# Layer A's group map multiplied into the u columns of the input projection on the chip, instead of a group product in every chunk

## Chip, cores and metric

The kernel runs on one core of one Trainium2 chip. The metric is the device time of one execution in microseconds, given as the median of several runs; a profiled execution, taken by the hardware profiler, has its own time.

## What is computed

A two-layer encoder trunk over 2048 tokens of width 1024. Layer 0 is the one that the change touches:

```python
def pool_mixer(h, w_in, w_group, scale, w_out):
    u, z = jnp.split(h @ w_in, 2, axis=-1)
    u = u.reshape(B, S, N_POOL_GROUPS, POOL_GROUP_DIM)      # 4 groups of 256
    cs = jnp.cumsum(u, axis=1)
    for g, w in enumerate((2, 4, 8, 16)):                   # trailing mean over w tokens
        means.append((cs[:, :, g] - cs shifted by w) / min(position, w))
    pooled = stack(means) - u
    mixed = einsum('bsgc,gcd->bsgd', pooled, w_group).reshape(B, S, 1024) * scale
    return (mixed * silu(z)) @ w_out
```

Here `h` is the RMS-normed input. The pooling works along the tokens and the group map along the channels of one group, so the two can change places: mapping u first and pooling afterwards gives the same values but for rounding. The layer's output is added to the stream, then a gated embedding `(p @ ple_w) * sigmoid(x @ ple_gate_w)` is added. A key/value projection follows, and layer 1 is a stick-breaking attention over 16 heads with its own projections.

## The kernel before, in words

All products run as three float32r matmuls (high x high, low x high, high x low): every operand is split into a rounded high part and a low remainder, a `pair` of two 128x512 tiles. Activations lie with channels on the partitions and 512 tokens along the free axis. `split` (L168) makes a pair: ACT copies the high part, another engine subtracts.

The first half of the program works on four chunks of 512 tokens, one after the other. A chunk is a list of 22 steps: for the groups 3, 2, 1, 0 a u step (`run_u`) and a z step (`run_z`), four steps of the output projection (`run_o`), four of the gated embedding (`run_g`), and six for q, k and v (`run_kvq`). One step's product of 1024 input channels is 8 x 2 x 3 = 48 matmuls of 128x512 on TensorE (`product`, L119). The weights of step i + 1 are requested before step i runs (L533), into a ring of 12 weight pairs (`wpair`, 512 KB each) that raw tiles (`wraw`, 3 of 256 KB) feed. `load_w` (L85) splits weights on ACT and DVE (L107, L108, with the norm's gain multiplied in) or ACT and POOL or DVE (L101, L103). The pairs of the layer's input projection are written to DRAM in the first chunk (L112, tensor `wi`), and later chunks load these pairs (L96).

A u step scales the product by the token's norm (`ub`, L230), forms the trailing sums in 1 to 4 shifted additions (`us`, L236, on DVE or POOL), takes mean minus itself (`po`, L240) and splits it into the pair `pp` (L247). The group product `run_m` (L268) multiplies `pp` by the group map, 2 x 2 x 3 = 12 matmuls of 128x512; it runs one u step later (for group 0 after the last z step). Its result is scaled, multiplied by SiLU(z) (`mf`, L275) and split into the pair `mp`, the operand of the output projection. `run_o` takes the `mp` pairs in the order 6, 7, 4, 5, 2, 3, 0, 1.

Beside the steps, the loads of the next chunk's input (`load_x`, `prep`) and the splitting of weights that the second half needs (`keep`, tiles `kraw` and `kpair`) are put in between. A scheduler orders the instructions of each engine within these dependences; an engine then runs its own list in order. SP issues most DMAs, also in order. The second half is the attention with layer 1's projections, from about 1415 us on.

## Time and profile before

| | us |
|---|---|
| median of 3 runs | 2865.52 |
| lowest, highest | 2864.01, 2867.44 |
| profiled execution | 2867.54 |
| its span, first to last instruction | 2865.7 |

The profile's page gives busy time by engine: PE is TensorE's matmuls, PEld its weight loads, DVE VectorE, ACT ScalarE, POOL GpSimd, SP the engine that issues DMAs. Further views used here: groups of instructions by line and shape (`line engine op out<-in shapes xcount | busy us, mean ns of one | idle time of the engine before them and what ended it`); windows (`from:to length, busy time and count by engine, clock, DMA share, GB/s`); waits (`engine line waited for: us in all, times, longest`); the timeline (`start us, duration us, engine, line, op, tiles, count`, in brackets the idle time before and what ended it). L353 is the line of the q, k, v products, L202 that of the input transposes, L598 and L599 are products of the attention, L623 its transposes.

### The profile page before, as it was taken

Reading aid. Unit: us, or ns where it says so; the run is one execution under the profiler, and the core shown is the slowest. Engines: PE = TensorE matmul, PEld = TensorE weight load, DVE = VectorE, ACT = ScalarE, POOL = GpSimd, SP = SyncE. Lnnn points to the kernel's source line nnn. Section 1 sums busy time; section 2 is a strip of 40 time slices with the busy share of each in tenths; the row PEclk is TensorE's granted clock in tenths of the full one; section 3 lists DMA queues with packets and bytes.
Section 4 is the critical chain, followed back from the end, with each engine's and each line's share of the span. In section 5 each row is a group of like instructions: output and inputs, shape, how many; then the busy total and the mean of one; then the engine's idle time right before and its main releaser. Section 6 shows DMA issues by size and latency. Waiting matters only on the chain. (4 is left out here: it accounts for less than half of the span.)

```text
span 2865.7 us, 40527 instructions
## 1 busy us (share of the span) xinstructions
PE 2763.3 (96%) x13667; PEld 2273.2 (79%) x13667; DVE 1893.8 (66%) x2581; ACT 1405.6 (49%) x2765; POOL 956.2 (33%) x965
## 2 busy tenths in 40 slices
PE   8899999999999999999899999999999999999999
PEld 6688788888888888888777888787877778878877
DVE  5645535455355543555299989999999988886642
ACT  4444523355234542345255555656566655554431
POOL 3464347542474425743212121221111122213220
PEclk9999999999999999999999999999999999999999
DMA  7756696467955678446657565555555556667765
GB/s 265 257 162 216 220 305 208 143 205 250 306 160 169 223 243 287 136 153 207 212 188 229 163 216 170 159 164 177 165 161 161 163 176 193 186 188 243 251 207 158
DMA packets 335139, 576.43 MB, mean 201 GB/s; under 512 B 32782, under 2 KB 161838, under 8 KB 334932
## 3 DMA queue, kind: packets, MB, share of 16 engines
q1 hardware_dynamic: 327944, 564.34, 61.2%
q10 hardware_dynamic: 6988, 9.50, 1.1%
q8 instruction: 108, 1.77, 0.3%
q14 instruction: 99, 0.81, 0.1%
HBM read 433.16 MB, written 132.19 MB: 197 GB/s over the span
## 5 line engine op out<-in xcount | busy, mean ns | idle before, releaser
L353 PE MATMUL psd<-wpair,x 128*128 128x512 f32 x2304 | 544.8, 393 | 0.0
L602 ACT ACTIVATE kap<-psl 128x512 f32<-128x512 f32 (+3 forms) x640 | 340.3, 533 | 407.6 <-PE psl L599 398.3
L609 DVE TENSOR_TENSOR_SCAN pp<-kap,pp,zeros 128x512 f32<-128x512 f32 x384 | 512.2, 1338 | 23.3 <-ACT kap L602 21.2
L353 PEld LDWEIGHTS psd<-wpair,x 128*128 128x128 f32 x2304 | 428.8, 188 | 86.4
L623 PE MATMUL psa<-ident,pp 128*128 128x128 f32 x2176 | 348.7, 275 | 42.7 <-DVE at L627 37.9
L627 DVE TENSOR_TENSOR at<-psa,at 128x512 fp32r<-128x512 f32 (+3 forms) x640 | 373.5, 586 | 14.8 <-ACT at L626 13.8
L623 PEld LDWEIGHTS psa<-ident,pp 128*128 128x128 f32 x2176 | 263.5, 141 | 127.0 <-DVE at L627 71.2
L626 ACT CAST at<-psa 128x512 fp32r<-128x512 f32 (+3 forms) x640 | 331.3, 519 | 51.7 <-PE psa L623 48.5
L604 POOL TENSOR_SCALAR_AFFINE_SELECT kap<-kap 128x128 f32<-128x128 f32 x256 | 88.0, 345 | 633.1 <-ACT kap L602 597.9
L609 DVE TENSOR_TENSOR_SCAN pp<-kap,zeros 128x128 f32<-128x128 f32 (+3 forms) x256 | 214.2, 838 | 93.7 <-POOL kap L604 92.4
L598 PE MATMUL psl<-kk,qa 128*128 128x512 f32 (+3 forms) x640 | 235.0, 367 | 7.0 <-ACT vr L390 5.2
L635 PE MATMUL pso<-at,vv 128*128 128x512 f32 (+3 forms) x640 | 235.2, 367 | 0.8 <-ACT at L626 0.7
L599 PE MATMUL psl<-kk,qb 128*128 128x512 f32 (+3 forms) x640 | 235.1, 367 | 0.0
L636 PE MATMUL pso<-at,vv 128*128 128x512 f32 (+3 forms) x640 | 234.1, 366 | 0.0
L126 PE MATMUL psd<-xp,wpair 128*128 128x512 f32 x512 | 201.2, 393 | 4.3 <-DVE wpair L108 4.2
L124 PE MATMUL psd<-xp,wpair 128*128 128x512 f32 x512 | 201.0, 393 | 3.6 <-ACT xp L169 2.4
L108 DVE SCALAR_TENSOR_TENSOR wpair<-wraw,gains,wpair 128x512 fp32r<-128x512 f32 x192 | 149.5, 790 | 82.1 <-ACT wpair L107 81.8
L125 PE MATMUL psd<-xp,wpair 128*128 128x512 f32 x512 | 200.7, 392 | 0.0
L107 ACT ACTIVATE wpair<-wraw,gains 128x512 fp32r<-128x512 f32 x192 | 136.8, 720 | 121.0 <-DMA wraw<-in_w_kv_dram 65.9
L103 POOL TENSOR_TENSOR wpair<-wraw,wpair 128x512 fp32r<-128x512 f32 x107 | 147.7, 1388 | 78.5 <-ACT wpair L101 58.8
L101 ACT CAST wpair<-wraw 128x512 fp32r<-128x512 f32 x160 | 96.1, 619 | 124.1 <-DMA wraw<-in_a_w_out_dram 51.5
L598 PEld LDWEIGHTS psl<-kk,qa 128*128 128x128 f32 x640 | 120.9, 189 | 28.7 <-ACT vr L390 5.7
(204 smaller groups left out, 5553.4 us busy)
## 6 DMA issues: line engine op xcount, KB each, us to landing
wpair<-wi SPq DMA_DIRECT2D x96, 512.0 KB
kk<-kd SPq DMA_DIRECT2D x320, 128.0 KB
vv<-vd SPq DMA_DIRECT2D x160, 256.0 KB
wraw<-in_w_kv_dram SPq DMA_DIRECT2D x128, 256.0 KB
wpair<-wzd SPq DMA_DIRECT2D x64, 512.0 KB
wpair<-wod SPq DMA_DIRECT2D x64, 512.0 KB
wpair<-wgd SPq DMA_DIRECT2D x64, 512.0 KB
wi<-wpair SPq DMA_DIRECT2D x32, 512.0 KB
```

The costliest lines, as they stand in the source:

```text
L124: T.matmul(ps, wst(units, kt, 0, c0), acts[kt][:, 0], start=(kt == order[0]), stop=False)
L126: T.matmul(ps, wst(units, kt, 1, c0), acts[kt][:, 0], start=False, stop=(kt == order[-1]))
L353: T.matmul(pss2[i], ck["x2"][kt][:, xh, tk], wst(ws, kt, wh, 0, W5), start=(kt == 0 and xh == 0 and wh == 0), stop=(kt == KT - 1 and wh == 1))
L598: T.matmul(ps[:, :w], qa[:, qs], kk[:, :w], start=True, stop=False)
L599: T.matmul(ps[:, :w], qb[:, qs], kk[:, :w], start=False, stop=True)
L602: A.activation(out=kp[:, r0:], in_=ps[:, :w], func=AF.Sigmoid, scale=-1.0)
L609: V.tensor_tensor_scan(out=pp[:, r0:][:, ::-1], data0=kp[:, r0:][:, ::-1], data1=zeros.to_broadcast([P, w]), initial=1.0 if st["diag"] els ...
L623: T.transpose(pt[:, j * P : (j + 1) * P], pp[:, r0 + kt * P : r0 + (kt + 1) * P], ident)
L626: A.copy(out=at[:, 0, cs], in_=pt[:, cs])
L627: V.tensor_tensor(out=at[:, 1, cs], in0=pt[:, cs], in1=f(at[:, 0, cs]), op=ALU.subtract)
L635: T.matmul(po[:, cs], vv[:, kt, :], at[:, 0, cs], start=(st["diag"] and kt == 0), stop=False)
L636: T.matmul(po[:, cs], vv[:, kt, :], at[:, 1, cs], start=False, stop=(st["last"] and kt == 3))
```

## The change

The group map is multiplied into the u columns of the input projection, once, on the chip, while the first chunk runs (`fold`). For each group the 1024 x 256 raw u columns are loaded (`load_fold`, tile `uraw`), turned by 16 transposes of 128x128 (tile `wt`, split into pairs) and multiplied by the group map in 4 x 12 matmuls of 128x256; the result is scaled by the norm's gain, split into weight pairs on ACT and DVE and written to DRAM in the place of the old u pairs. The pieces of a fold are put between the matmuls of the same group's z product. So the z step now comes ahead of the u step of a group, in all chunks, and the u step of the first chunk loads no weights. `run_m` and the split `pp` are gone from all chunks: `run_u` multiplies the pooled tile by the scale and SiLU(z) and splits it into `mp` itself. Steps behind group 0: the u step is now the last before the output projection.

```diff
-    def product(pss_, units, acts, c0s, order=None):
+    def product(pss_, units, acts, c0s, order=None, beside=()):
+        beside = iter(beside)
         for kt in order:
             for ps, c0 in zip(pss_, c0s):
...
+            next(beside, None)
+        for _ in beside:
+            pass

+        def load_fold(g):
+            raws = []
+            if g == 3:
+                wg = load_w(wp, a_w_group[0, g], 2, 0, 256)[0]
+                for p0 in range(0, KT, 4):
+                    raw = f(pair("uraw"))
...
+            for p0 in range(0, KT, 2):
+                raw = io.tile([P, 2, 256], F32, tag="io", name="uraw")
+                nc.sync.dma_start(out=raw, in_=...)   # u columns of group g
+                raws.append(raw)
+            return raws, load_w(wp, a_w_group[0, g], 2, 0, 256)[0]

+        def fold(g, raws, wg):
+            units = chunk[0].setdefault("wu", {})[g] = []
+            wts = []
+            def across(i):
+                pt = turned()
+                for ct in range(2):
+                    for e in range(2):
+                        T.transpose(pt[:, 2 * ct + e, :], raws[i][:, e, ct * P : (ct + 1) * P], ident)
+                wt = pair("wt")
+                split(wt, pt.rearrange("q j t -> q (j t)"), V)
+                wts.append(wt)
+            def mapped(i):
+                ps = dense()
+                for e in range(2):
+                    n = 0
+                    for ct in range(2):
+                        ks = slice((2 * ct + e) * P, (2 * ct + e + 1) * P)
+                        for wh, gh in ((0, 0), (0, 1), (1, 0)):
+                            T.matmul(ps[:, e * 256 : (e + 1) * 256], wts[i][:, wh, ks], wg[:, gh, ct, :],
+                                     start=(n == 0), stop=(n == 5))
+                            n += 1
+                pr = wpair.tile([P, 2, 2, 256], F32R, tag="wpair", name="wpair")
+                for e in range(2):
+                    ga = g_a[:, 2 * i + e : 2 * i + e + 1]
+                    A.activation(out=pr[:, 0, e], in_=ps[:, e * 256 : (e + 1) * 256], func=AF.Identity, scale=ga)
+                    V.scalar_tensor_tensor(out=pr[:, 1, e], in0=ps[:, e * 256 : (e + 1) * 256], scalar=ga,
+                                           in1=f(pr[:, 0, e]), op0=ALU.mult, op1=ALU.subtract)
+                units.append(pr)
+                d = split_once["wi", g * 256, 2 * i] = dram.tile([P, 2, 2, 256], F32, name=f"wu_{g}_{i}")
+                nc.sync.dma_start(out=d, in_=f(pr))
+            for i in range(4):
+                across(i)
+                yield
+                if i:
+                    mapped(i - 1)
+                    yield
+            mapped(3)
+            yield

         def run_z(s, g, wz):
-            product(pss2, wz, ck["x"], (0, P))
+            product(pss2, wz, ck["x"], (0, P), beside=fold(g, *ck["fold"].pop(g)) if not s else ())
+            settle()
+            if "rb" not in ck:
+                ck["rb"] = bcast(ck["r"], "x")
...
-        def run_u(s, g, wu, wg=None):
+        def run_u(s, g, wu):
-            product(pss2, wu, ck["x"], (0, P))
+            product(pss2, wu or ck["wu"].pop(g), ck["x"], (0, P))
...
-                pp = pair("pp")
-                split(pp, po, V)
-                pooled.append(pp)
+                V.scalar_tensor_tensor(out=po, in0=po, scalar=g_s[:, o : o + 1], in1=ck["zs"][g][k],
+                                       op0=ALU.mult, op1=ALU.mult)
+                pr = pair("mp")
+                split(pr, po, G)
+                ck["m"][o] = pr
-        def run_m(s, g, wg):
-            product(pss2, wg, ck["pooled"].pop(g), (0, P))
...
+                steps.append((lambda load=load: load(z=1), lambda *w, s=s, g=g: run_z(s, g, *w)))
                 steps.append((load, lambda *w, s=s, g=g: run_u(s, g, *w)))
-                steps.append((lambda load=load: load(z=1), lambda *w, s=s, g=g: run_z(s, g, *w)))
```

More of the change, by code (lines that the diff above doesn't have):

```diff
@@ L170, in split, with settle @@
             lo.tensor_tensor(out=pr[:, 1], in0=src, in1=f(pr[:, 0]), op=ALU.subtract)
-        chunk = [{"zs": {}, "pooled": {}, "m": {}} for _ in range(NSUB)]
+        lag = []
+        late = []
+        def settle():
+            while late:
+                late.pop(0)()
+        chunk = [{"zs": {}, "m": {}, "fold": {}} for _ in range(NSUB)]
         def load_x(s):
@@ L220, in run_u, with run_z @@
+        def run_z(s, g, wz):
+            ck = chunk[s]
             pss2 = [dense(), dense()]
-            product(pss2, wu, ck["x"], (0, P))
+            product(pss2, wz, ck["x"], (0, P), beside=fold(g, *ck["fold"].pop(g)) if not s else ())
             settle()
@@ L224, in run_u @@
                 ck["rb"] = bcast(ck["r"], "x")
-            pooled = []
+            zs = []
+            for k in range(2):
+                zr, sg = tmp("zr"), tmp("sg")
+                V.tensor_tensor(out=zr, in0=pss2[k], in1=ck["rb"], op=ALU.mult)
+                A.activation(out=sg, in_=zr, func=AF.Sigmoid)
+                G.tensor_tensor(out=zr, in0=zr, in1=sg, op=ALU.mult)
+                zs.append(zr)
+            ck["zs"][g] = zs
+        def run_u(s, g, wu):
+            ck, win = chunk[s], WIN[g]
+            pss2 = [dense(), dense()]
+            product(pss2, wu or ck["wu"].pop(g), ck["x"], (0, P))
             for k in range(2):
@@ L524, in trunk_kernel @@
         ready = steps[0][0]()
+        chunk[0]["fold"][3] = load_fold(3)
         state["first"] = False
```

51 lines of the change are left out of this document (15 added, 36 removed).

## The prediction, made before the changed kernel ran

> **What bounds the kernel now.** I read the page's busy shares and slices first, then a table of windows cut at the stage borders, then who TensorE waited for, then single stretches of the timeline.
>
> ```profile
> PE 2763.3 (96%) x13667; PEld 2273.2 (79%) x13667; DVE 1893.8 (66%) x2581; ACT 1405.6 (49%) x2765; POOL 956.2 (33%) x965
> ...
> PE   8899999999999999999899999999999999999999
> ...
> PEclk9999999999999999999999999999999999999999
> DMA  7756696467955678446657565555555556667765
> ```
>
> TensorE is busy in 96% of the span, and its clock is full nearly throughout. Only the first two of the 40 slices and the one at the border to attention stand at 8. So a matmul less is time less, wherever TensorE doesn't wait; the other engines count only where they make it wait. The change touches the u and z products of layer A and what follows them, so I cut there: the first chunk up to its first output projection, the rest of that chunk, and the u/z stages of the three later chunks.
>
> ```profile
> 0.00:132.50 132.50, 112.87 (x471) 88.61 (x472) 83.79 (x189) 61.91 (x139) 48.92 (x58) 0.97 0.77 265
> 132.50:383.90 251.40, 246.21 (x1122) 202.63 (x1122) 128.83 (x179) 120.79 (x215) 116.65 (x95) 0.99 0.63 208
> 383.90:482.30 98.40, 98.40 (x437) 81.44 (x436) 46.20 (x66) 30.69 (x59) 59.94 (x58) 1.00 0.80 273
> 727.30:826.50 99.20, 98.98 (x437) 81.39 (x436) 50.81 (x68) 31.39 (x62) 59.36 (x58) 1.00 0.80 271
> 1072.50:1172.70 100.20, 98.99 (x438) 81.38 (x437) 43.45 (x66) 31.14 (x59) 59.12 (x57) 1.00 0.75 256
> ```
>
> The columns are length, busy PE, PEld, DVE, ACT, POOL, clock, DMA share, GB/s. The later u/z stages (98.4, 99.2, 100.2 us) are solid TensorE work. The first chunk's stage is not: 19.6 of 132.5 us are idle, at a clock of 0.97 and a DMA share of 0.77.
>
> **What a TensorE instruction costs.** Durations overlap, so the price is the distance between starts.
>
> ```profile
> 383.89 0.39 PE L124 MATMUL psd<-xp,wpair 128*128 128x512 f32 x1
> 1399.70 11.27 PE L353 MATMUL psd<-wpair,x 128*128 128x512 f32 x49
> L623 PE MATMUL psa<-ident,pp 128*128 128x128 f32 x2176 | 348.7, 275 | 42.7 <-DVE at L627 37.9 <-DVE ple L741 1.6 <-DVE pp L609 1.4
> 20.72 1.03 PE L202 MATMUL pst<-ident,xin 128*128 128x128 f32 x8
> 1457.19 0.28 PE L598 MATMUL psl<-kk,qa 128*128 128x256 f32 x1
> 1457.31 0.28 PE L599 MATMUL psl<-kk,qb 128*128 128x256 f32 x1
> ```
>
> 49 matmuls over 512 columns take 11.27 us, the last 0.39 of it: (11.27 - 0.39)/48 = 0.227 us each. Eight transposes take 1.03, the last 0.275 of it (the mean of one, third row): 0.755/7, about 0.109 each. Two matmuls over 256 columns start 0.12 apart.
>
> **Part 1: the group products go.**
>
> ```profile
> L125 PE MATMUL psd<-pp,wpair 128*128 128x512 f32 x64 | 26.0, 406 | 2.4 <-DVE pp L170 2.4
> L124 PE MATMUL psd<-pp,wpair 128*128 128x512 f32 x64 | 25.7, 402 | 1.4 <-ACT pp L169 1.4
> L126 PE MATMUL psd<-pp,wpair 128*128 128x512 f32 x64 | 25.6, 400 | 0.0
> ```
>
> 3 x 64 = 192 matmuls, 48 a chunk, 48 x 0.227 = 10.9 us a chunk. A u/z stage has 384 others: 384 x 0.227 = 87.2 us. If the later stages become that, they give 98.4 - 87.2, 99.2 - 87.2 and 100.2 - 87.2: 11.2 + 12.0 + 13.0 = 36.2 us. The bounds: 32.7 (the matmuls alone, their waits kept) and 36.2. So much if the hand-over to the output projection, now straight behind u, holds. Today's chain behind a u of the first chunk (start, us; window of 16, then the ends of the next group's), and the means of what follows it:
>
> ```profile
> 32.75 1.29 DVE L230 TENSOR_TENSOR ub<-psd,rbx 128x512 f32<-128x512 f32 x2 [3.05 <-ACT rbx L165]
> 33.95 0.70 DVE L236 TENSOR_TENSOR us<-ub 128x527 f32<-128x527 f32 x1
> 34.73 2.26 POOL L236 TENSOR_TENSOR us<-us 128x525 f32<-128x525 f32 x2
> 37.19 0.68 DVE L236 TENSOR_TENSOR us<-us 128x513 f32<-128x513 f32 x1
> 38.19 0.68 DVE L240 SCALAR_TENSOR_TENSOR po<-us,ub 128x512 f32<-128x512 f32 x1
> 47.02 0.68 DVE L170 TENSOR_TENSOR pp<-po,pp 128x512 fp32r<-128x512 f32 x1
> ...
> 57.28 1.28 DVE L230 TENSOR_TENSOR ub<-psd,rbx 128x512 f32<-128x512 f32 x2
> 73.32 0.68 DVE L170 TENSOR_TENSOR pp<-po,pp 128x512 fp32r<-128x512 f32 x1
> ```
>
> ```profile
> L169 ACT CAST xp<-pst 128x512 fp32r<-128x512 f32 x32 | 18.3, 582 | 15.4 <-PE pst L202 13.7 <-DMA ve<-vr 0.9 <-issue 0.3
> L275 DVE SCALAR_TENSOR_TENSOR mf<-psd,gains,zr 128x512 f32<-128x512 f32 x32 | 23.3, 743 | 11.8 <-POOL zr L262 11.8
> L170 POOL TENSOR_TENSOR mp<-mf,mp 128x512 fp32r<-128x512 f32 x32 | 47.2, 1489 | 14.9 <-ACT mp L169 14.9
> ```
>
> In the later chunks the last group has a window of 2, one sum and none on POOL. After the last u product DVE does two `ub`, two sums, two `po` and two scalings, ACT casts and POOL subtracts: by these rows 1.28 + 2 x 0.70 + 2 x 0.68 + 2 x 0.74 = 5.5, then 0.6 and 1.5, about 8 us for the first of the pair and 9 for the second. The projection takes the last group's `mp` last, after 36 matmuls (8.2 us), and the second one's after 42 (9.5). It just fits; I charge 0.5 us a chunk. So **-34.7 us**.
>
> **Part 2: the first chunk pays.** The fold adds, for each of 4 groups, 16 transposes and 48 matmuls over 256 columns: 64 x 0.109 + 192 x 0.12 = 7.0 + 23.0 = 30.0 us, against 10.9 saved: **+19.1 us** of TensorE work. [...]
>
> On the other engines the fold mostly replaces work:
>
> ```profile
> L107 ACT ACTIVATE wpair<-wraw,g_a 128x256 fp32r<-128x256 f32 x64 | 27.9, 500 | 34.4 <-DMA wraw<-in_a_w_in_dram 34.4
> L108 DVE SCALAR_TENSOR_TENSOR wpair<-wraw,g_a,wpair 128x256 fp32r<-128x256 f32 x64 | 35.6, 602 | 35.7 <-ACT wpair L107 35.7
> L170 DVE TENSOR_TENSOR xp<-pst,xp 128x512 fp32r<-128x512 f32 x32 | 21.6, 683 | 5.1 <-ACT xp L169 5.1
> ```
>
> The 8 scalings a group (L107, L108) now read PSUM instead of loaded weights, same count and size. New are 4 splits a group (0.58 on ACT, 0.68 on DVE, as the casts and splits of `xp`); the 2 splits of `pp` a group go. That is under 1.5 us a group on either engine, both below two thirds busy in that stage. The scale-and-gate (L275) only changes its input. DMA: the raw u columns (4 MB) and the stored pairs (8 MB) are moved as before; 12 of 16 loads of the group map and their splits go.
>
> The waits of this stage decide more. What TensorE waited for in the first 132.5 us, beside the start (us in all, times, longest):
>
> ```profile
> PE psd L126 <- DVE wpair L108: 4.2, 3, 2.3
> ...
> PE psd L125 <- DVE pp L170: 2.0, 1, 2.0
> PE psd L124 <- ACT wpair L107: 1.2, 1, 1.2
> ```
>
> The wait for `pp` has no object any more. Those for weights came from loads behind the stores; with 19 us more work to the same bytes they shrink. I let all go: -7.4 (bounds -7.4 and 0). In their place comes a new wait. In the changed kernel's instruction order the splits of a fold's first transposes stand on ACT and DVE behind the whole pooling chain of the previous u, and TensorE meets the first fold matmul after some 38 z matmuls and 8 transposes: 38 x 0.227 + 0.9 = 9.5 us after that u. The other z matmuls of the step are queued behind it. By the chain rows above it takes today, from the first `ub` to the last `pp`, 14.9 us, in the next group 16.7, with weight scalings in between. Without those it is 1.3 + 0.7 + 2.3 + 0.7 + 0.7 + 0.2 for the first half, 0.7 + 2.3 + 0.7 + 0.7 + 0.2 + 0.7 for the second, then two ACT casts, 1.2: 12.4 us. So TensorE waits 12.4 - 9.5 = 3 us, and with weight scalings kept in the queue up to 16.7 - 9.5 = 7 us. Three groups meet it (the first fold has no u ahead). I take 3 each, **+9 us**, bounds 0 and 21: the built order puts only 4 scalings into the stretch, and for windows of 8 and 4 the POOL sums are fewer.
>
> Sum for the first chunk: 19.1 - 7.4 + 9 = +20.7, bounds 19.1 - 7.4 = +11.7 and 19.1 + 21 = +40.
>
> **The number.** -34.7 + 20.7 = -14 us. The profiled execution took 2867.5 us (span 2865.7 and 1.8 around it); the median shown is 2865.5, 2.0 lower. So 2865.5 - 14 = **2851.5 us**. A measurement can tell about 0.2%, 5.7 us, from no change. With the bounds of the first chunk alone 2842.5 to 2871. The second half (attention) is untouched and just starts earlier.
>
> **Rivals.** (1) *The first chunk swallows the fold.* Beyond its work it waits 27.4 us today (132.5 - 64 x 0.109 - 432 x 0.227): the 7.4 above, the rest at the start and through the clock. If the first fold fills some 6 us of that rest, and the chain is met in time, the chunk costs 19.1 - 7.4 - 6 = +5.7, and the time is 2836.5. For it: there are holes to fill, and DMA gets more time for the same bytes. Against: the fold needs loads of its own at the start. Chance 0.15.
>
> (2) *The fold waits behind loads, and the kernel gets slower.* Scalings of z weights and of kept weights stand between the pooling chain and the fold's splits, in order on ACT and DVE; each blocks until its load has landed. The 16.7 us chain has 4.3 more than its own work; with twice that it is 21, the wait 11.5 a group. And such a wait costs twice, since the clock drops:
>
> ```profile
> 1422.01 0.77 PE L664 MATMUL psd<-x,wpair 128*128 128x512 f32 x1 [3.81 <-DMA wpair<-wzd]
> ...
> 1425.53 0.40 PE L668 MATMUL psd<-x,wpair 128*128 128x512 f32 x1
> ```
>
> After 3.81 us idle, eight matmuls (first and ninth start shown) take 3.52 us instead of 1.82: 1.7 lost. 3 x (11.5 + 1.7) = 39.6, the 5.4 us of weight waits stay, and the chunk costs 19.1 - 2.0 + 39.6 = +56.7, net +22, 2887.5. It decides from (34.7 - 19.1 + 2.0)/3 = 5.9 us a group, the clock's share included: below, the change gains. For it: both chains shown are that long. Against: the built order leaves few scalings in the stretch. Chance 0.12, a third of it near the break-even point.
>
> (3) *DMA bounds the later stages.* They move 98.4 us x 273 GB/s = 26.9 MB, and now have 87 us for nearly as much. At 273 GB/s less 0.25 MB for each of four maps that takes 95 us: 3.5 us gained a chunk instead of 11, net about +10, 2875; half of it 2863. Against: TensorE has no idle time in 383.9 to 482.3, and over 20 us between the issue of weights and their use (first matmul: 383.89 above):
>
> ```profile
> 356.81 3.53 SPq L96 DMA_DIRECT2D wpair<-wi  x3
> ```
>
> Chance 0.08. (4) *Transposes cost their 275 ns*, if between other matmuls they don't overlap as they do among themselves: 64 x (0.275 - 0.109) = +10.6, 2862. Against: they stand in fours. Chance 0.05.
>
> **How the numbers follow.** The forecast has 0.60, with its own range 2842 to 2860 (new waits between none and twice what I took). To hold 8 in 10 the range takes in the upper half of (1), all of (4), half of (3) and the break-even part of (2): 2836 to 2868. Faster by over 0.2% (below 2859.8): 0.58 of the forecast and 0.15 of (1), 0.73. Within 0.2% (to 2871.2): 0.02 of the forecast, 0.05 of (4), 0.04 each of (2) and (3), 0.15. Slower: 0.08 of (2) and 0.04 of (3), 0.12.
>
> **What would show it.** In the changed kernel's profile: no matmul reading `pp`; the three later u/z stages at 87 to 89 us with TensorE full; fold matmuls 0.12 and transposes 0.11 apart; the first output projection at about 153 us instead of 132.5; and three waits of a few us at the first fold matmul, ended by ACT or DVE `wt`. I am wrong if the later stages stay above 91 us (DMA), or if these waits exceed 6 us a group.

## The result: 0.3% slower, where 0.5% faster was forecast

The changed kernel takes 2877.18 us (median of 6 runs, 2871.39 to 2880.89) against 2866.61 us before, on the same chip (6 runs, 2864.01 to 2867.44): ratio 1.0034, 95% interval 1.0024 to 1.0044. The forecast was 2851.5 us in a range of 2836 to 2868. The profiled execution took 2872.49 us, 5.0 more than that of before.

The page's busy shares and the windows of the changed kernel, cut at the same borders: the first chunk up to its first output projection, then for each chunk the output projection, and between them the u/z stages of chunks 1 to 3 (length, busy PE, PEld, DVE, ACT, POOL, clock, DMA share, GB/s). The second block has the four output projections of the kernel before:

```profile
PE 2755.6 (96%) x13731; PEld 2274.6 (79%) x13731; DVE 1888.6 (66%) x2561; ACT 1389.7 (48%) x2737; POOL 938.7 (33%) x957
...
0.00:161.10 161.10, 133.89 (x679) 112.99 (x680) 87.93 (x191) 69.61 (x153) 52.14 (x59) 0.95 0.68 238
161.10:211.40 50.30, 46.98 (x194) 37.87 (x192) 25.46 (x33) 17.15 (x29) 34.06 (x27) 0.93 0.36 116
411.80:499.30 87.50, 87.50 (x390) 72.45 (x389) 35.45 (x54) 25.13 (x50) 54.79 (x52) 1.00 0.83 297
499.30:549.90 50.60, 46.35 (x193) 37.59 (x192) 23.43 (x27) 15.61 (x26) 32.38 (x27) 0.93 0.32 104
749.60:837.10 87.50, 87.50 (x390) 72.45 (x389) 39.35 (x55) 26.30 (x53) 54.53 (x54) 1.00 0.84 297
837.10:888.20 51.10, 46.31 (x193) 37.46 (x192) 23.48 (x27) 15.85 (x27) 33.18 (x27) 0.93 0.32 103
1088.20:1175.70 87.50, 87.50 (x389) 72.46 (x388) 37.71 (x51) 25.28 (x50) 56.83 (x55) 1.00 0.81 283
1175.70:1221.60 45.90, 44.38 (x193) 35.84 (x193) 23.73 (x27) 14.56 (x25) 28.49 (x22) 1.00 0.31 103
```

```profile
132.50:181.00 48.50, 46.03 (x193) 36.89 (x193) 20.84 (x26) 19.75 (x35) 37.24 (x28) 0.96 0.55 174
482.30:527.80 45.50, 44.14 (x194) 35.84 (x193) 18.02 (x23) 16.73 (x28) 31.93 (x24) 1.00 0.36 115
826.50:871.90 45.40, 44.45 (x194) 35.84 (x193) 21.23 (x24) 16.64 (x29) 32.13 (x24) 1.00 0.37 117
1172.70:1216.20 43.50, 43.50 (x193) 35.96 (x192) 18.78 (x22) 15.84 (x28) 31.33 (x24) 1.00 0.37 115
```

The three later u/z stages gave what was forecast: 87.5 us each, TensorE busy throughout. Two other things ate it. The first chunk's stage grew by 28.6 us instead of 20.7. And the four output projections, 48.5, 45.5, 45.4 and 43.5 us before, are now 50.3, 50.6, 51.1 and 45.9: 15.0 us more in all, where the prediction charged 1.5. With -35.3 from the u/z stages that is +8.3; the other stages give 3.3 back. TensorE's busy share is the same 96% as before: the share doesn't tell a kernel that waits less from one that waits elsewhere.

Who TensorE waits for in these stages (us in all, times, longest), first in 0 to 161.1, then from there to 1222:

```profile
PE psd L273 <- ACT wt L174: 13.1, 3, 4.9
...
PE psd L126 <- ACT mp L174: 8.6, 4, 3.2
PE psd L127 <- POOL mp L175: 5.2, 4, 1.9
```

L273 is the fold's map product. L126 and L127 are the first two of the three matmuls on a k tile (128 input channels); the first reads the high part of the activations, the second the low part. Here they belong to the output projection, which stands still for the last pairs of `mp`: 13.8 us in all. The hand-over from the last u product to the output projection in chunk 1, on VectorE, ScalarE, GpSimd and TensorE (the u product ends at 499.3):

```profile
502.55 1.33 DVE L103 TENSOR_TENSOR wpair<-wraw,wpair 128x512 fp32r<-128x512 f32 x1 [5.37 <-ACT wpair L101]
503.80 1.27 DVE L320 TENSOR_TENSOR ub<-psd,rbx 128x512 f32<-128x512 f32 x2
505.00 2.41 DVE L326 TENSOR_TENSOR us<-ub 128x527 f32<-128x527 f32 x2
507.33 1.28 DVE L330 SCALAR_TENSOR_TENSOR po<-us,ub 128x512 f32<-128x512 f32 x2
508.54 1.40 DVE L336 SCALAR_TENSOR_TENSOR po<-po,gains,zr 128x512 f32<-128x512 f32 x2
...
501.89 0.62 ACT L101 CAST wpair<-wraw 128x512 fp32r<-128x512 f32 x1 [0.18 <-DMA wraw<-in_a_w_out_dram]
509.31 1.28 ACT L174 CAST mp<-po 128x512 fp32r<-128x512 f32 x2 [2.48 <-DVE po L336]
...
498.29 2.54 POOL L307 TENSOR_TENSOR zr<-zr,sg 128x512 f32<-128x512 f32 x2
500.79 2.55 POOL L103 TENSOR_TENSOR wpair<-wraw,wpair 128x512 fp32r<-128x512 f32 x2
511.04 1.25 POOL L175 TENSOR_TENSOR mp<-po,mp 128x512 fp32r<-128x512 f32 x1
...
509.98 0.50 PE L126 MATMUL psd<-mp,wpair 128*128 128x512 f32 x1 [2.39 <-ACT mp L174]
512.35 0.80 PE L127 MATMUL psd<-mp,wpair 128*128 128x512 f32 x1 [1.87 <-POOL mp L175]
```

VectorE doesn't touch the u product until 503.80, 4.5 us after its end. It stands at a low part of the output projection's own weights (L103), and that waits for ScalarE's cast (501.89 to 502.51), which itself waited for the raw weights, as the cast ahead of it had (2.40 us, until 501.10). Then the two sums (`us`) take 1.2 us each instead of 0.7. The first late `mp` pair's high part is there at 509.9, its low part at 512.3. GpSimd starts that low part only at 511.0, after a low part of the weights. The matmuls on the six `mp` pairs formed earlier had lasted to 507.6.

### The profile page after: what moved, and what is told of

It is laid out like the page before. It is cut to its first block, busy times and chain, and to the rows that moved or that the text cites. A ratio compares the mean times of both kernels' runs of the same rounds, so it can differ in the third digit from the quotient of the medians.

```text
span 2870.7 us, 40538 instructions
## 1 busy us (share of the span) xinstructions
PE 2755.6 (96%) x13731; PEld 2274.6 (79%) x13731; DVE 1888.6 (66%) x2561; ACT 1389.7 (48%) x2737; POOL 938.7 (33%) x957
## 5 line engine op out<-in xcount | busy, mean ns | idle before, releaser
L664 DVE TENSOR_TENSOR_SCAN pp<-kap,pp,zeros 128x512 f32<-128x512 f32 x384 | 512.2, 1339 | 22.6 <-ACT kap L657 20.6
L682 DVE TENSOR_TENSOR at<-psa,at 128x512 fp32r<-128x512 f32 (+3 forms) x640 | 373.7, 586 | 14.9 <-ACT at L681 13.8
L126 PE MATMUL psd<-xp,wpair 128*128 128x512 f32 x512 | 201.8, 394 | 2.7 <-ACT xp L174 2.7
L127 PE MATMUL psd<-xp,wpair 128*128 128x512 f32 x512 | 200.8, 392 | 0.0
L108 DVE SCALAR_TENSOR_TENSOR wpair<-wraw,gains,wpair 128x512 fp32r<-128x512 f32 x192 | 151.1, 799 | 73.3 <-ACT wpair L107 72.9
L103 POOL TENSOR_TENSOR wpair<-wraw,wpair 128x512 fp32r<-128x512 f32 x99 | 135.6, 1373 | 107.5 <-ACT wpair L101 80.7
L101 ACT CAST wpair<-wraw 128x512 fp32r<-128x512 f32 x148 | 89.7, 619 | 135.3 <-PE psd L128 89.0
```

Of the source, the lines that this page charges most:

```text
L126: T.matmul(ps, wst(units, kt, 0, c0), acts[kt][:, 0], start=(kt == order[0]), stop=False)
L127: T.matmul(ps, wst(units, kt, 0, c0), acts[kt][:, 1], start=False, stop=False)
L664: V.tensor_tensor_scan(out=pp[:, r0:][:, ::-1], data0=kp[:, r0:][:, ::-1], data1=zeros.to_broadcast([P, w]), initial=1.0 if st["diag"] els ...
L682: V.tensor_tensor(out=at[:, 1, cs], in0=pt[:, cs], in1=f(at[:, 0, cs]), op=ALU.subtract)
```

## The experiments

Each time is a median; behind it stand its ratio to the kernel before, run again on the same chip (2866.0 to 2868.6 us), and the 95% interval. The changed kernel was not timed again beside the experiments, so a difference from its 2877.18 us can hold some 2 us of the chips' own. Stages are read from the profiles, one execution each. A single stage differs between profiles of the same hand-over: the first output projection takes 50.3 us in the changed kernel, 45.5 and 45.7 in experiments 9 and 13, the last one 45.9, 50.5 and 50.3. The sum of the four is steadier: 197.9 in the changed kernel, 197.5, 199.4 and 198.5 in experiments 1, 9 and 13, which leave the hand-over as it is.

**1. All of the next fold's transposes beside the previous u product.** The map products stay beside z.

```diff
             for i in range(4):
                 across(i)
                 yield
-                if i:
-                    mapped(i - 1)
-                    yield
-            mapped(3)
-            yield
+            for i in range(4):
+                mapped(i)
+                yield
...
-            product(pss2, wu or ck["wu"].pop(g), ck["x"], (0, P))
+            ahead = ()
+            if not s and g:
+                going = ck.setdefault("going", {})[g - 1] = fold(g - 1, *ck["fold"].pop(g - 1))
+                ahead = (next(going) for _ in range(4))
+            product(pss2, wu or ck["wu"].pop(g), ck["x"], (0, P), beside=ahead)
```

> From the changed kernel; the 16 transposes of a group's fold and their splits are put beside the u product of the group before, ahead of its pooling chain on ACT and DVE. Theory A (the fold's matmuls wait for wt behind the pooling chain, 13.1 us in three waits, each followed by matmuls at half clock): the three waits go, the first chunk's u/z stage falls from 161 to about 145 us, the o stages keep their 50, 51, 51, 46 us, and the time is 13 to 17 us under the changed kernel's 2877: about 2862. Rival B (the first chunk is bound by its loads and splits, the waits only show where TensorE stands): as much waiting comes back elsewhere in the stage, mostly for weights; under 5 us gained.

2875.22 us, 1.0027 (1.0017 to 1.0037), not the 2862 of theory A. The wait changed its place; in the first chunk's stage:

```profile
PE pst L261 <- DVE wt L175: 9.6, 3, 6.2
```

The third group of transposes needs a PSUM buffer back, and the splits that free it stand behind scalings of weights: in experiment 3, with the same edit, four of them (L108) start at 48.59 us on VectorE, and the first `wt` split at 51.94. The stage fell by 4.0 us, the output projections stayed at 50.9, 51.1, 50.0 and 45.6.

**2. Output steps merged.** The first two steps take the six early `mp` pairs of both blocks first, the two late pairs after. The same matmuls, with 8.2 us more of them ahead of the late pairs.

```diff
+            if b == 0:
+                part(pss2, wo, ck["m"], (6, 7, 4, 5, 2, 3), True, False)
+                ck["o0"] = pss2, wo
+                return
+            if b == 1:
+                part(pss2, wo, ck["m"], (6, 7, 4, 5, 2, 3), True, False)
+                ps0, wo0 = ck.pop("o0")
+                part(ps0, wo0, ck["m"], (0, 1), False, True)
+                close_o(s, 0, ps0)
+                part(pss2, wo, ck["m"], (0, 1), False, True)
+                close_o(s, 1, pss2)
+                return
...
```

> From the changed kernel; the first two steps of the output projection take the six early mp pairs of both column blocks first and the two late ones after that, so TensorE meets the late pairs 16.4 us after the last u product instead of 8.2. Theory A (what is lost in the later chunks is the hand-over from the last u product to the output projection, 13.8 us of waits in four chunks plus half clock): no wait for mp, o stages of about 44 us each in place of 50, 51, 51, 46, and 13 to 18 us less: about 2862. Rival B (the splits of the output weights are what is late, the mp wait only comes first): a wait for wpair takes its place, under 5 us gained.

2850.67 us, 0.9940 (0.9928 to 0.9953), 26.5 under the changed kernel, where theory A gave 13 to 18. Windows of its first two output projections:

```profile
161.90:205.50 43.60, 43.60 (x194) 36.03 (x194) 23.68 (x32) 16.86 (x30) 31.64 (x26) 1.00 0.39 122
494.20:537.70 43.50, 43.50 (x193) 35.97 (x192) 23.43 (x27) 15.46 (x26) 32.92 (x27) 1.00 0.36 115
```

All four are 43.5 or 43.6 us, TensorE full, clock 1.00: 174.1 together instead of 197.9. Of these 23.8 us, 13.8 were waits; the other 10 go with the clock, 0.93 in three stages of some 50 us. The work is the same and only its order changed, so the order of the products decides whether the late hand-over costs anything.

**3. Both edits, of experiments 1 and 2.** 

> Both edits, transposes early and the two first output steps merged. Theory A (two separate waits): the gains add, 26 to 35 us under the changed kernel, 2842 to 2851, and 16 to 25 us under the kernel before. Rival B: under 8 us gained, no better than the kernel before by more than noise.

2850.53 us, 0.9941 (0.9927 to 0.9954): nothing on top of the second. The output projections start 4.1, 4.6, 4.8 and 2.5 us earlier than in experiment 2, and the span ends 1.0 us earlier: what the first chunk gains is kept up to the third output projection and given back behind it. No run here shows why.

**4. Without the group map.** Nothing is folded and no group product is left; u's columns are loaded and split as before, in the changed kernel's order of z and u.

```diff
-            product(pss2, wz, ck["x"], (0, P), beside=fold(g, *ck["fold"].pop(g)) if not s else ())
+            product(pss2, wz, ck["x"], (0, P))
-                    if not s and z and g < 3:
-                        chunk[0]["fold"][g] = load_fold(g)
-                    if not s and not z:
-                        return (None,)
...
```

> From the changed kernel without the fold: the group map is left out altogether, the u columns are loaded and split in the first chunk as in the kernel before; z before u and the mp split straight behind u are kept. It shows what the fold itself costs. Theory A (hand-over and fold waits are separate losses): the o stages keep their 50, 51, 51, 46 us; the first chunk's u/z stage is 94 us of work plus some 20 of start and weight waits, 114 to 120 in place of 161; the time is 41 to 47 us under the changed kernel, about 2833. Rival C (the o stages are late because the fold has pushed loads back): they fall to 44 to 46 us also, and the time is about 2820.

2833.24 us, 0.9882 (0.9868 to 0.9895), as theory A had it. The output projections are still 47.8, 52.4, 49.9 and 44.0 us (the first waits 3.9 us for weights): the late hand-over of the later chunks doesn't come from the fold.

**5. u ahead of z again in chunks 1 to 3,** the pairs formed in z's step.

```diff
-                steps.append((lambda load=load: load(z=1), lambda *w, s=s, g=g: run_z(s, g, *w)))
-                steps.append((load, lambda *w, s=s, g=g: run_u(s, g, *w)))
+                pair_ = [(lambda load=load: load(z=1), lambda *w, s=s, g=g: run_z(s, g, *w)),
+                         (load, lambda *w, s=s, g=g: run_u(s, g, *w))]
+                steps += pair_[::-1] if s else pair_
...
```

> Chunks 1 to 3 run u before z within each group again (the group map stays in u's columns), so the step ahead of the output projection is z, and the gated pairs are formed in z's step. Theory A (the pairs are late because VectorE stands, in its own order, behind the low parts of the output weights, which wait for their transfer): whatever step stands last is late, the output stages of chunks 1 to 3 stay near 50.6, 51.1 and 45.9 us, and the time stays within 4 us of 2877. Rival B (u's chain of window sum, pooling, gate and split is simply too long for the last step): z's chain is as short as before, the three stages fall to 45.5, 45.4 and 43.5 us, some 13 us less in all, and the time is near 2864.

2876.31 us, 1.0036 (1.0022 to 1.0049), stages 49.9, 48.4 and 49.5. Here z is the last step, and it is late as u was. Before the change z was last as well, but the 12 matmuls of the group product (12 x 0.227 = 2.7 us) stood between it and the output projection. z's chain starts 5.5 to 5.6 us behind its product in both (485.09 behind 479.6 before, 505.97 behind 500.4 here). So what differs is mainly the cover of 2.7 us, and the change took that away with the work. The rest of the chain differs less: the first high part is finished 10.2 us behind z's product before (489.8) and 11.4 here (511.8).

**6. Low parts of the output weights all on GpSimd.**

```diff
-                (G if state["w"] % 3 else V).tensor_tensor(out=pr[:, 1], in0=raw, in1=f(pr[:, 0]), op=ALU.subtract)
+                (G if state["w"] % 3 or pool else V).tensor_tensor(out=pr[:, 1], in0=raw, in1=f(pr[:, 0]), op=ALU.subtract)
...
```

> Only the engine of one operation changes: the low parts of the output projection's weights (line 103), of which every third ran on VectorE, all run on GpSimd, so VectorE's queue holds nothing that waits for those weights. Theory A (VectorE blocked in order): VectorE takes up the last u product as it ends, the wait for ScalarE's mp (8.6 us, 4 times) falls under 3 us, the wait for GpSimd's mp may grow by up to 4 us since GpSimd has more to do; output stages fall by 2 to 4 us each, the time to 2865 to 2872. Rival B (the chain itself is too long): the waits for mp stay above 12 us in all, output stages within 1 us of 50.3, 50.6, 51.1 and 45.9, time 2875 to 2880.

2880.55 us, 1.0047 (1.0034 to 1.0060): theory A's 2865 to 2872 was missed. VectorE and GpSimd at the hand-over of chunk 1 (the output projection starts at 502.2):

```profile
501.68 1.37 DVE L320 TENSOR_TENSOR ub<-psd,rbx 128x512 f32<-128x512 f32 x2 [4.44 <-PE psd L128]
502.97 2.79 DVE L326 TENSOR_TENSOR us<-ub 128x527 f32<-128x527 f32 x2
505.69 3.48 DVE L330 SCALAR_TENSOR_TENSOR po<-us,ub 128x512 f32<-128x512 f32 x2
509.09 2.44 DVE L336 SCALAR_TENSOR_TENSOR po<-po,gains,zr 128x512 f32<-128x512 f32 x2
...
502.18 3.02 POOL L307 TENSOR_TENSOR zr<-zr,sg 128x512 f32<-128x512 f32 x2
505.14 5.17 POOL L103 TENSOR_TENSOR wpair<-wraw,wpair 128x512 fp32r<-128x512 f32 x3
```

VectorE does take up the product at once, as A said. But its `us`, `po` and gate take 1.2 to 1.7 us each beside a GpSimd that is busy without a break, where 0.7 is their own time, and the chain ends as late as ever.

**7. The kernel before the change, with merged output steps.** It has the edit of experiment 2.

> The kernel before the change, with only the output steps merged as in the second experiment: the first two take the six early mp pairs of both blocks first and the late two after. It prices the hand-over that was there already. Theory A (the change made the hand-over worse, by 15 us in its profile): the output stages fall from 48.5, 45.5, 45.4 and 43.5 us to 43.5 each, so 9 us come off: 2858, and the changed kernel with the same merge (2850.7) stays 7 to 8 us ahead, which is the change with the hand-over left out. Rival B (the merge is worth the same whatever the group map does): some 26 us come off, 2840, and the change loses 10 us even with a clean hand-over.

2863.98 us, 0.9987 (0.9979 to 0.9996): 6 us over theory A's 2858, and far from rival B's 2840. The projections of chunks 1 to 3 fell to 43.5; that of chunk 0 stayed late at 49.8, with a wait of 3.2 us for weights. So the merge takes 4.4 us off the kernel before, and 26.5 off the changed kernel. With the merge in both, the change gains 2863.98 - 2850.67 = 13.3 us.

**8. Experiment 4 with merged output steps.** 

> No fold and no group product anywhere (the group map is left out, so the outputs are not the reference's), with the merged output steps. Against the second experiment (2850.7) it prices the fold alone with a clean hand-over. Theory A (the fold costs what chunk 0's stage shows, 162 us against 124, and is independent of the hand-over): 38 us plus 4 us of reloading in the second chunk, so 2809 to 2813. Rival B (the fold hides part of waits that come back without it, for weights in chunk 0): 2818 or more.

2818.13 us, 0.9829 (0.9817 to 0.9842): 32.5 under experiment 2, as rival B said. The first output projection starts 38.0 us earlier (123.9 against 161.9). Of these, 4.0 are lost within it, which waits for its own weights, split by ScalarE:

```profile
PE psd L363 <- ACT wpair L101: 3.8, 1, 3.8
```

**9 and 10. First map product behind the seventh k tile of z,** in the changed kernel (9) and in experiment 2 (10). One `yield` goes to each k tile of the z product.

```diff
+            if g < 3:
+                across(0)
+                yield
+                across(1)
+                yield
+                for _ in range(4):
+                    yield
+                mapped(0)
+                yield
+                across(2)
+                yield
+                mapped(1)
+                across(3)
+                mapped(2)
+                mapped(3)
+                return
```

> Only the place of the fold's first products changes (groups 2, 1, 0): the first two turns stay behind the first two k tiles of the z product, but the first map product comes only behind the seventh k tile (5.4 us of TensorE work later), the other turns and products behind that. Theory B (the 13.1 us of fold waits are lost because the turned pairs are split behind the whole chain of the u product before, and TensorE gets to them too early): the three waits of 4.9 us go, chunk 0's u/z stage falls from 161.1 to 145 to 149 us, the late pairs at the output projection stay (50 us a stage), and the time falls by 12 to 16 us to 2861 to 2865. Theory A (the wait only moves, since the later turns and the u product then stand behind the same queues): the stage stays above 156 us and the time above 2872.

> The late fold together with the merged output steps of the second experiment. If the two losses are independent, the gains add: output stages of 43.5 us, chunk 0's u/z stage 145 to 149 us, time 2836 to 2840. If the fold's waits only move, or what is gained early is given back to weights that then come late, as in the third experiment: 2848 to 2851.

2868.13 us, 1.0005 (0.9993 to 1.0018), and 2848.43 us, 0.9929 (0.9916 to 0.9941). The fold waits fell only to 10.5 and 9.1 us. The expectation was wrong about the start: the scheduler had the first map product behind the sixth k tile already, so this moved it by one, 1.3 us. In the profile of experiment 9 the first stage still ends at 161.0 us, and the profiled execution took 2872.67 us against 2872.49; the median is 9.0 us lower all the same, and no profile here shows where. In experiment 10 the first stage ends 3.7 us earlier than in experiment 2, and the time is 2.2 lower.

**11. Weights of the first output step asked for one step earlier.**

```diff
-            after = steps[i + 1][0]() if i + 1 < len(steps) else None
+            step, s = i % STEPS, i // STEPS
+            after = early if step == 7 else steps[i + 1][0]() if i + 1 < len(steps) else None
+            if step == 6:
+                early = steps[i + 2][0]()
...
```

> The first output step's weights are asked for and split one step earlier (beside the last z step instead of the last u step), so neither VectorE's nor GpSimd's queue holds weight work ahead of or beside the last u chain; the order of the products is as in the changed kernel. Theory A (the late pairs come from that weight work: first VectorE standing behind it, and when it is all on GpSimd, VectorE's instructions running at half speed beside it): the chain then takes seven VectorE instructions of 0.7 us, one of ScalarE of 0.6 and one of GpSimd of 1.3, 6.8 us, less than the 8.2 us of the six early pairs; the output stages fall to 43.5 to 45 us, 18 to 24 us off with their clock, 2852 to 2860. Rival B (the chain is late whatever stands beside it): stages stay near 50 us, 2873 to 2881.

2878.48 us, 1.0032 (1.0020 to 1.0045), stages 49.1, 50.4, 53.0 and 47.4. It didn't do what it was meant to. At the hand-over of chunk 1 VectorE stands at the same place, for the same reason:

```profile
505.49 1.47 DVE L103 TENSOR_TENSOR wpair<-wraw,wpair 128x512 fp32r<-128x512 f32 x1 [5.23 <-ACT wpair L101]
506.88 1.27 DVE L320 TENSOR_TENSOR ub<-psd,rbx 128x512 f32<-128x512 f32 x2
```

Asked for earlier, the weights were not split earlier; whether these are the first or already the second step's, the rows don't tell. So the time, which is rival B's, says nothing for rival B or against it.

**12. Low parts of the output weights all on VectorE,** the edit of experiment 6 the other way round.

```diff
-                (G if state["w"] % 3 else V).tensor_tensor(out=pr[:, 1], in0=raw, in1=f(pr[:, 0]), op=ALU.subtract)
+                (G if state["w"] % 3 and not vec else V).tensor_tensor(out=pr[:, 1], in0=raw, in1=f(pr[:, 0]), op=ALU.subtract)
...
```

> The other way round from the experiment that put all low parts of the output weights on GpSimd: all four of each step run on VectorE, none on GpSimd. VectorE then stands behind all of them, but GpSimd is free and cannot slow it. Theory A1 (standing in order is what counts): VectorE takes up the last u product later than 4.5 us after its end, output stages 52 us or more, 2880 to 2888. Theory A2 (sharing with GpSimd is what counts): the u chain's instructions take 0.7 us each instead of 1.2 to 1.7, stages 46 to 49 us, 2862 to 2872.

2858.52 us, 0.9963 (0.9950 to 0.9977), 18.7 under the changed kernel and better than either theory, with stages of 45.1, 44.3, 45.7 and 43.5. VectorE and GpSimd at the same hand-over (u ends at 498.1):

```profile
495.95 3.42 DVE L103 TENSOR_TENSOR wpair<-wraw,wpair 128x512 fp32r<-128x512 f32 x3 [0.67 <-ACT wpair L101]
499.28 1.28 DVE L320 TENSOR_TENSOR ub<-psd,rbx 128x512 f32<-128x512 f32 x2
500.48 1.31 DVE L326 TENSOR_TENSOR us<-ub 128x527 f32<-128x527 f32 x2
501.72 1.28 DVE L330 SCALAR_TENSOR_TENSOR po<-us,ub 128x512 f32<-128x512 f32 x2
502.92 1.40 DVE L336 SCALAR_TENSOR_TENSOR po<-po,gains,zr 128x512 f32<-128x512 f32 x2
...
504.40 4.01 POOL L175 TENSOR_TENSOR mp<-po,mp 128x512 fp32r<-128x512 f32 x2 [0.68 <-ACT mp L174]
```

More work for VectorE, and yet it starts 1.2 us after the product instead of 4.5, its sums take 0.65 us, and GpSimd is free when the pairs come. With GpSimd's share of the weights gone, VectorE stands for less and its chain is faster; of the 13.8 us of waits for `mp` 2.6 are left. This speaks for theory A2, but not for it alone: VectorE's standing, which A1 was about, fell as well.

**13 and 14. Two groups of transposes ahead.** Only `across(0)` and `across(1)` go beside the previous u product (two PSUM buffers, splits ahead of u's chain); `mapped(0)`, `mapped(1)` and the other turns follow behind the first k tiles of z, the last two maps behind z. In the changed kernel (13) and in experiment 2 (14).

```diff
+            if g < 3:
+                for piece in (across, 0), (across, 1), (mapped, 0), (mapped, 1), (across, 2), (across, 3):
+                    piece[0](piece[1])
+                    yield
+                for _ in range(4):
+                    yield
+                mapped(2)
+                mapped(3)
+                return
...
+                ahead = (next(going) for _ in range(2))
```

> Of each later fold only the first two groups of four transposes are done beside the previous group's u product, so their splits stand ahead of that u's pooling chain on VectorE and ScalarE (in the built order too), and the two PSUM buffers are enough; the first two map products come right at the start of the z product, the last two only behind it. Theory B (the 13.1 us of fold waits come from splits that stand behind the u chain): no wait for wt of over 1 us is left, the 20-us slices of this stage stay at full clock, the u/z stage of the first chunk falls from 161.1 to 144 to 148 us, and the time by 10 to 17 us to 2860 to 2867, with the late pairs at the output projection as they are. Theory A (the fold must wait for loads one way or another): the wait moves to the map group or the raw u columns, the stage stays above 155 us and the time above 2872.

> The same, with the merged output steps of the second experiment. Theory B: 2850.7 less 13 to 17 us, 2834 to 2838, with output stages of 43.5 us; both terms that the prediction undersized are then gone, and what is left is the work of the fold against that of the group products. Theory A: 2848 to 2851, as the third experiment.

2867.43 us, 1.0002 (0.9993 to 1.0011), and 2840.62 us, 0.9915 (0.9901 to 0.9928), the fastest of all. Experiment 13 ends its first stage at 153.2 instead of 161.1, short of the 144 to 148 expected. Its output projections take 45.7, 50.2, 52.4 and 50.3 us, as much in all as in the changed kernel. The window of experiment 14's first stage, and what TensorE waits for there at the fold's map products:

```profile
0.00:151.10 151.10, 131.93 (x680) 110.00 (x681) 82.28 (x192) 69.37 (x154) 51.52 (x60) 0.98 0.74 253
...
PE psd L273 <- ACT wt L174: 4.9, 3, 3.1
```

The stage is 10.8 us shorter than in experiment 2 and the time 10.0. Of the 13.3 us of fold waits 4.9 are left, now at the map products behind z. The expected 13 to 17 us was too much by about that rest. The waits shrink when the splits of the turned pairs go ahead of u's chain, and those that are left stand at the pairs still split behind it; so the place of the splits makes the waits.

**15. Four raw weight tiles instead of three.**

```diff
-        wraw = st.enter_context(tc.tile_pool(name="wraw", bufs=3))
+        wraw = st.enter_context(tc.tile_pool(name="wraw", bufs=4))
```

> The changed kernel with four raw weight tiles instead of three, nothing else. If the late start of the last u chain comes from the ring (GpSimd, 1.3 to 1.8 us for each low part and busy without a break, holds the raw tiles, so the next transfers start late and VectorE's low part ahead of the u chain waits for them), the transfer has one tile more in hand, VectorE takes up the u product 1.5 to 3 us after its end instead of 4.5, the output stages fall by 2 to 3 us each, 2864 to 2871. If the transfers are late for another reason (their bandwidth, or the stores ahead of them in SP's queue), the stages stay at 50.3, 50.6, 51.1 and 45.9 within 1 us: 2874 to 2880.

2866.39 us, 0.9996 (0.9987 to 1.0005), 10.8 under the changed kernel. VectorE now starts 2.9 us after the product's end:

```profile
498.00 0.86 DVE L103 TENSOR_TENSOR wpair<-wraw,wpair 128x512 fp32r<-128x512 f32 x1 [5.87 <-ACT wpair L101]
498.78 1.28 DVE L320 TENSOR_TENSOR ub<-psd,rbx 128x512 f32<-128x512 f32 x2
```

(The product ends at 495.85.) So the ring is part of it: with one raw tile more in hand VectorE's low part, and u behind it, come 1.6 us sooner. That GpSimd, with 1.27 to 1.78 us for each low part, is what holds the tiles is read from its unbroken row in the changed kernel and from experiment 12, not shown by itself. The stages, 50.8, 48.5, 49.1 and 44.5, fell by 5.0 us in all; the rest of the gain isn't in them.

## Why the prediction was wrong, step by step

**The group products (-36.2): right.** Measured 98.4 + 99.2 + 100.2 - 3 x 87.5 = 35.3 us. The rival that transfers bound these stages falls: TensorE is full in them at 283 to 297 GB/s, more than the 273 that it took for a limit.

**The hand-over ("It just fits; I charge 0.5 us a chunk"): the step that failed.** It was charged with +1.5 us. The profiles show +15.0, and by the merge it is 26.5 us in the changed kernel against 4.4 before: +22.1, which is 20.6 of the miss of 25.7. The chain of 8 us was summed from mean durations and begun at the product's end. Its length was about right: in chunk 1 it takes 8.5 us, from 503.8 to the low part at 512.3. Its start was wrong, 4.5 us late where the slack was 0.2. The sum left out three things. In VectorE's queue a weight's low part stands ahead of u and waits for a transfer. VectorE's two sums are slower beside a busy GpSimd (2.41 us, against 1.31 in experiment 12), and GpSimd comes to the `mp` low part late (1.1 us). And with TensorE's waits of 2.4 and 1.9 us the clock falls as well (0.55 in 510 to 515 us). The row that should have warned was in the profile of before, on VectorE at the same place in the same chunk:

```profile
484.37 0.79 DVE L103 TENSOR_TENSOR wpair<-wraw,wpair 128x512 fp32r<-128x512 f32 x1 [3.42 <-ACT wpair L101]
485.09 1.27 DVE L260 TENSOR_TENSOR zr<-psd,rbx 128x512 f32<-128x512 f32 x2
```

z's product had ended at 479.6 there, and the group product's 2.7 us lay over part of the delay.

**The fold waits (+9) were mis-sized:** they are 13.1 us, and behind two of the three the clock falls (0.54 in 69 to 74 us, 0.50 in 105 to 110, 1.00 behind the third). The same work (24 map products, 8 transposes and one matmul over 512 columns) takes 4.0 us behind the third wait and 6.2 behind each of the other two. The mechanism was the forecast one. In the first case 14.5 us pass from `ub` (54.2) to the first matmul on `wt` (68.8), not 12.4. VectorE's scalings of loaded z weights account for about 0.6 us of this; more comes from GpSimd, which puts a copy of 0.7 us between its sums, and beside which VectorE's last sum takes 1.74 us instead of 0.68:

```profile
64.03 1.74 DVE L326 TENSOR_TENSOR us<-us 128x513 f32<-128x513 f32 x1 [1.10 <-POOL us L326]
...
63.96 1.26 POOL L175 TENSOR_TENSOR mp<-po,mp 128x512 fp32r<-128x512 f32 x1
```

The prediction also read the pooling wrong: GpSimd has two sums for a window of 8, as for 16, and one only for 4. The waits are 4.6, 4.9 and 3.6 us for 16, 8 and 4. With the clock that makes (13.1 + 2 x 2.2)/3 = 5.8 us a group, about half of rival 2's 13.2 and just short of the 5.9 from which the fold alone would have made the kernel slower.

**The rest of the first chunk.** The work (+19.1) and the old waits (-7.4) have no experiment each. Their sum, +11.7, stands against experiments 14 and 7, where most fold waits are out and the output steps are the same: 151.1 - 130.1 = +21.0. Of these 4.9 are fold waits that are left, and 2.0 a new wait for a split of the input at the start. The other 14.1 hold the clock's loss around the 3.1 us wait too (0.64 in 70 to 75 us of experiment 14). The old waits for `pp` and for z's weights are gone from the list.

**The transposes** don't cost here the 275 ns that one lasts (L623 in the profile of before). In the first chunk of the changed kernel, four of them and the matmul behind:

```profile
57.88 0.60 PE L261 MATMUL pst<-ident,uraw 128*128 128x128 f32 x4
58.23 0.47 PE L126 MATMUL psd<-xp,wpair 128*128 128x512 f32 x1
```

It is 0.35 us from start to start, and the next matmul starts 0.31 us behind that one (58.54) instead of 0.227: some 0.11 us for each transpose, as forecast. So the rival that charged them 10.6 us falls.

**The sum.** With the merge in both kernels the change gains 13.3 us; without its charge for the hand-over the forecast was 15.5. That they are this near is in part luck. Between the profiles of experiments 7 and 2 the first chunk's u/z stage grows by 31.8 us, 11 more than forecast. Against it stand 6.2 us in the first output projection, which waits for its weights in experiment 7 (49.8 against 43.6), and some 4 in the stages between; neither was in the forecast. The number failed by a wait that the change made on the other side of the stage, where the slack was 0.2 to 0.5 us on paper, and the paper had no queue in it. No rival said so: all four looked at the stages in which matmuls were added or removed. And neither sign of being wrong that the prediction named came: the later stages are at 87.5 us, and no fold wait exceeds 4.9.

Three things stay open. Why the raw weights come late is shown only in part (experiment 15). The medians differ by 10.6 us, the profiled executions by 5.0. The changed kernel's runs spread over 9.5 us, those of experiment 2 over 1.7; experiment 15's eleven spread over 6.6, the three with a mean clock of 0.992 taking 2861.8 to 2862.8 and those at 0.990 and 0.991 2864.3 to 2868.4. That fits waits that sometimes cost the clock and sometimes not, but experiment 7 spreads by 7.6 without late pairs in three chunks, and no run was made that holds the clock. And how much of experiment 12's gain is the earlier start and how much the faster chain wasn't separated; in chunk 1 the start is 3.3 us earlier and the two sums are 1.1 us faster.

## What to carry to other kernels

When a change removes work between two stages, what lay behind it loses its cover: take the chain of the step that is then last, in the order in which each engine's queue really runs it, weights of the next step included, and compare it with the work that stands ahead of its result. A hand-over that is short of slack was mended here by order (partial sums over what is ready, for two blocks, then the rest; 26.5 us), and for the most part by taking weight work off the slowest engine in it (GpSimd, with a mean of 1.37 us for a low part of the weights in the changed kernel, VectorE 1.06; 18.7 us). And a fix that frees one queue by loading another engine has to be judged with both running.

## What the runs showed of the hardware

**VectorE beside GpSimd.** In experiment 6 `ub`, which reads one operand from PSUM, keeps its 0.68 us while GpSimd works; `us` and `po`, with two operands in SBUF, take 1.40 and 1.74 there, against 0.65 and 0.64 in experiment 12, where GpSimd has only copies of 16 columns beside them (500.03 to 503.7 us). In these rows it is the operations with two SBUF inputs that slow down. Why they do, and how long one engine waits for the other, can't be read from them.

**When a wait costs the clock.** Windows of 5 us in the changed kernel: around its third fold wait (3.57 us idle before 140.24), and around the hand-over of chunk 1 (2.39 and 1.87 us idle, shown above):

```profile
140.00:145.00 5.00, 4.76 (x36) 4.57 (x37) 2.96 (x6) 3.20 (x8) 1.51 (x2) 1.00 0.35 99
...
510.00:515.00 5.00, 3.13 (x7) 2.32 (x8) 1.71 (x1) 1.63 (x3) 5.00 (x4) 0.55 0.32 104
515.00:520.00 5.00, 5.00 (x18) 3.97 (x17) 2.47 (x3) 1.25 (x2) 3.30 (x4) 0.77 0.17 57
```

The longer wait left the clock at 1.00; the two shorter ones, with one matmul between them, took it to 0.55. In windows of 2 us it is 1.00 from 508 to 510, 0.63 from 510 to 512 and 0.50 from 512 to 514, so it fell before the second wait was over. So the length of one wait doesn't tell here whether the clock falls: it stayed full behind the 3.57 us and had fallen within the 2.39 and 1.87. What decides it no run shows.
